# A streaming encoder trunk: the second block of frames turned once, the next frames' casts one per step, the pooled products later, one weight sum pinned

## The chip, the core and the metric

The kernel runs on one core of one Trainium2 chip. The metric is device microseconds of one execution. A TensorE matmul (PE) reads its operands from SBUF and adds into a bank of PSUM; VectorE (DVE) and ScalarE (ACT) prepare the operands and read the results; GpSimd (POOL) and SyncE (SP) mostly issue DMAs, and POOL computes a few small vectors. Each engine works off its own queue in order and waits on semaphores for the others.

## The reference

There are 2048 prompt frames and 32 sample frames of 1024 channels, and one layer:

```
proj = rmsnorm(h) @ w_in                   # 1024 -> 6 x 512: h, b, c, za, v, zb
u    = c * h ;  yA = b * (conv3(u) + bias) * silu(za)
pooled_g = (mean of the last 2/4/8/16 frames of v) - v        # four groups of 128 channels
yB   = (pooled_g @ pool_w_g) * pool_scale * silu(zb)
h    = h + concat(yA, yB) @ w_out
h    = h + (p @ w_ple) * sigmoid(rmsnorm(h) @ w_gate)
y    = rmsnorm(h)                          # and the last rows of u and v as new states
```

All inputs and outputs are fp32.

## The kernel before

**Tiling.** The 2080 frames are five blocks of 416, in groups [0, 1], [2, 3] and [4]. Channels run over the partitions, so the frames are loaded as rows, normalised (`normal`, L406) and turned by PE transposes through PSUM (`turn`, L413). fp32 products are made from pairs of parts: `split` casts a high part on ACT (L77) and subtracts it on DVE for the low part (L78), and each product is three matmuls (high x high, high x low, low x high). The trunk is: the projection by w_in (L556), the product with w_out (L162, L167), the embedding (L102), the gate, the last norm.

**Units.** The projection goes through four units of 128 columns of each of the six parts (h, b, c, za, v, zb) for each group. Unit 0 of group 0 is `plain`: six products for each block, zb, v, c, h, za, b. All other units of groups 0 and 1 are `seven`: three pairs (zb/v, c/h, za/b), each of which multiplies two blocks by two weights with seven half products (84 matmuls of 416 columns) instead of eight, as Strassen's scheme does. A `pair` is a generator of eight steps: weights, X with 11, Y with 12, X with the sum S2, Z with S1, X with S3, Z with S4, X with 22. `pair_weights` (L517) makes the sums of the raw weights on DVE (s_t is L536, the third sum is L533) and `make` splits them. X, Y and Z are PSUM banks (`ps_m`, six of them), emptied by ACT copies (`carry`, L851) and DVE additions (L854, L885). Group 1's unit 0 runs its zb/v and c/h pairs side by side, step for step. Group 2's four units are `plain` with one block.

**Frames for group 0.** Block 0's frames are turned at the start. `second_block` (L585) is a generator that `plain` calls between its products: it normalises block 1's frames, turns them into B0's parts 12 and 22 (pt1, in banks of `ps_m`), and later, for each of four column chunks (128, 128, 128 and 32 frames), turns the same frames a second time (pt2, in the two banks of `ps_t`), copies one half by ACT (L611) and forms the combinations T1, T2, T3, T4 with block 0's parts on DVE (L604). T4 goes to memory through a staging tile.

**Frames for group 1.** While units 1 to 3 run, `aside` is called 24 times a unit, at each step of each pair. It advances `next_columns(3, 0, 1, 2)` at a pace of 35 steps for 56 calls: for each column chunk, `frame_sums` (L431) takes the sums of squares on ACT (L88), normalises, turns, forms the sums f12, f1, f21 (L445 to L455) and stages each part: `to_memory` (L479) splits it into a staging tile of the ring `xin` (five buffers, shared with the loaded frames xt) and a POOL DMA stores it in p_d. The halves of the next chunk's frames are loaded by SP (L392) at its steps 5 and 7, counted from 0. `load_group(1)` loads the parts back by POOL.

**Pooling.** `pool_blocks` forms the trailing sums of v on DVE (L726, L735 to L738) and splits the result pl into pp. `mix` (L698) multiplies pp by pool_w, three matmuls for each block (L704 to L706), and DVE scales it into zs (L708); the result is stored in y_d by SP (L697).

**Order.** A scheduler orders the instructions of each engine's queue unless `keep_in_program_order` holds some of them in the order of the program. Before the change the turns of the next frames and the statistics of frames are so held.

Of the kernel before, what the change touches and what calls it, by code (L numbers as in the profile page):

```python
# [12 lines left out]
ALU = mybir.AluOpType  # L13
PSUM = bass.MemoryType.PSUM

P = 128
# [3 lines left out]
DEC = 32  # L20
# [7 lines left out]
NH = D // 2  # L28
KH = KC // 2
# [5 lines left out]
def trunk(ctx, tc, x_p, x_s, c_conv, c_pool, p_p, p_s, g_mix, w_in, conv_w, conv_b, pool_w,  # L35
          pool_scale, w_out, g_ple, w_gate, w_ple, g_fin, y_p, y_s, sc_p, sp_p, sc_s, sp_s):
    nc = tc.nc
# [38 lines left out]
    def split(hi, lo, src, eng=nc.vector):  # L76
        ins = nc.scalar.copy(hi, src)  # L77
        eng.tensor_tensor(lo, src, hi.bitcast(F32), op=ALU.subtract)  # L78
        return ins
# [250 lines left out]
    with ExitStack() as s1:  # L330
# [16 lines left out]

        def put(piece, src):

            split(piece[:, :, 0], piece[:, :, 1], src)  # L350

        def ftile(name):
            return wk.tile([P, KH, P], F32, tag="f", bufs=4, name=name)
# [42 lines left out]
        def x_stat(x, later=False):  # L396

            t, n, name = x
            return t, n, sumsq(t, n, name, later=later)
# [34 lines left out]
        def frame_sums(xs, tag, dst):  # L434

            xs = [x_stat(x, True) for x in xs]
            for x in xs:  # L440
                normal(x)
                yield
            n = P if len(xs) == 2 else DEC
            f12, f1, f21 = (ftile(f"{c}_{tag}")[:, :, :n] for c in ("f12", "f1", "f21"))
            sub = lambda o, x, y: nc.vector.tensor_tensor(o, x, y, op=ALU.subtract)  # L445
            steps = four(xs, tag)
            p11, p12 = next(steps)
            nc.scalar.copy(f12, p12)
            sub(f1, f12, p11)
            dst("11", p11, n)  # L450
            yield
            dst("T1", f1, n)
            yield
            p21, p22 = next(steps)
            nc.scalar.copy(f21, p21)  # L455
            sub(f1, p22, f1)
            sub(f12, p22, f12)
            dst("21", p21, n)
            yield
            dst("22", p22, n)  # L460
            yield
            dst("T2", f1, n)
            sub(f21, f21, f1)
            yield
            dst("T3", f12, n)
            yield
            dst("T4", f21, n)
            yield
# [7 lines left out]
        def staged(name):  # L476
            return xin.tile([P, KH, 2, P], F32R, tag="t", name=name)

        def to_memory(mem, name, src, at, n, t=None):  # L479
            t = t or staged(name)[:, :, :, :n]  # L480
            put(t, src)
            nc.gpsimd.dma_start(mem[:, :, :, at:at + n], t.bitcast(F32))

        def six(g):
# [39 lines left out]
        def pair_weights(gi, ka, kb, j, name, ring, s_ring):  # L524

            s_t = (wk.tile([P, KH, P], F32, tag="s", bufs=1, name=f"s_{name}") if s_ring is None else
                   s_ring(f"s_{name}"))  # L530
            ra = raw_weight(ka, j, f"{name}a", ring)
            a11, a12 = ra[:, :KH], ra[:, KH:]
            sub = lambda o, x, y: nc.vector.tensor_tensor(o, x, y, op=ALU.subtract)  # L533
            rb = raw_weight(kb, j, f"{name}b", ring)
            a21, a22 = rb[:, :KH], rb[:, KH:]
            nc.vector.tensor_tensor(s_t, a21, a22, op=ALU.add)  # L536
            sub(a21, a11, a21)
            s3 = a21
            src = {"11": a11, "12": a12, "S2": a11, "S1": s_t, "S3": s3, "S4": a12, "22": a22}

            def make(q):
                if q == "S2":
                    sub(a11, s_t, a11)
                if q == "S4":
                    sub(a12, a12, a11)
                t = wtile(f"w_{name}_{q}")
                put(t, src[q])
                return t

            return make  # L550
# [24 lines left out]
        B0 = {}  # L575
# [13 lines left out]
        def second_block():  # L589

            spans = [(c, slice(c * P, min(NB, c * P + P))) for c in range(4)]
            xs = []
            for c in range(3):
                x = x_tile(f"1_{c}", [x_rows(1, c)])
                normal(x)
                xs.append((x, slice(0, P)))
                yield
            xs.append((short0, slice(DEC, 2 * DEC)))
            for c, cs in spans:
                x = xs[c][0]  # L600
                for half, q in enumerate(("12", "22")):
                    put(B0[q][:, :, :, cs], turn(x, half, f"pt1_{c}_{half}", bank)[:, :, xs[c][1]])
                yield
            op = lambda o, a, b, op=ALU.subtract: nc.vector.tensor_tensor(o, a, b, op=op)  # L604
            for c, cs in spans:
                x, ts = xs[c]
                n = ts.stop - ts.start
                t1, t3, t2, t4 = (ftile(f"f{t}_1_{c}")[:, :, :n] for t in range(4))
                part = lambda q, h: B0[q][:, :, h, cs].bitcast(F32)
                p12 = turn(x, 0, f"pt2_{c}_0")[:, :, ts]  # L610
                nc.scalar.copy(t3, p12)  # L611
                op(t1, p12, part("11", 0))
                p22 = turn(x, 1, f"pt2_{c}_1")[:, :, ts]
                op(t3, p22, t3)
                op(t1, t1, part("11", 1))
                op(t2, p22, t1)
                put(B0["T2"][:, :, :, cs], t2)
                put(B0["T1"][:, :, :, cs], t1)
                put(B0["T3"][:, :, :, cs], t3)
                op(t4, part("21", 0), t2)  # L620
                op(t4, t4, part("21", 1), ALU.add)
                to_memory(p_d["T4"], f"T4_0_{c}", t4, c * P, n)
                yield
# [30 lines left out]
        class Unit:  # L654
# [98 lines left out]
            def plain(self):  # L753
# [73 lines left out]
                wb = weights("b", j, f"b{tag}")  # L827
                if self.last and j == 3:
                    early_embedding()
                for b in blocks:  # L830
                    ps = product_of("b", b, wb)
                    y = self.cols(c_s, b)
                    nc.vector.tensor_tensor(y, ps, y, op=ALU.mult)
                    self.store(j, b, c_s)
                if len(tbs) == 1:
                    self.turn_states(st)


            def pair(self, ka, kb, B, D, done, ring, s_ring=None):
# [39 lines left out]
            def seven(self, B, aside, both=False):  # L879
# [53 lines left out]
                while i < 3:  # L933
                    side_by_side = 2 if both and i == 0 else 1
                    if i <= 1 < i + side_by_side:
                        self.history(U, 2, halo_u, hist_u(j))
                    steps = [self.pair(*pairs[i + n], ring[i + n], ftile if n else None) for n in range(side_by_side)]
                    for _ in range(8):
                        for st in steps:
                            next(st)  # L940
                            aside()
                    for st in steps:
                        assert next(st, None) is None
                    i += side_by_side
                    if i - side_by_side <= 1 < i:
                        for b in range(2):
                            self.mix(b)

# [71 lines left out]
        def next_columns(*cs):  # L1020

            load_ahead(1, cs[0])
            for c, after in zip(cs, cs[1:] + (None,)):

                places = iter(t[:, :, :, i * DEC:(i + 1) * DEC] for t in map(staged, ("short_0", "short_1")) for i in range(4))
                dst = lambda q, src, n: to_memory(p_d[q], f"{q}_1_{c}", src, c * P, n, next(places) if n == DEC else None)
                for i, _ in enumerate(frame_sums(ahead.pop((1, c)), f"g1_{c}", dst)):
                    if after is not None and i in (5, 7):
                        load_half_ahead(after)
                    yield  # L1030

# [14 lines left out]
        def at_pace(steps, num, den):  # L1046

            calls = [0]

            def step():  # L1050
                calls[0] += num
                while calls[0] >= den:
                    calls[0] -= den
                    next(steps, None)

            return step

        B = B0
        for gi, tbs in enumerate(GROUPS):
# [17 lines left out]
            for j in range(4):  # L1077
                unit = gi * 4 + j
                u = Unit(gi, tbs, j)
                if unit == 0:  # L1080
                    u.plain()
                    B0["T4"] = piece_of(seventh("B0_T4"), 0)
                    nc.sync.dma_start(B0["T4"].bitcast(F32), p_d["T4"])
                    p_d["T4"] = tc.dram_tile([P, KH, 2, NB], F32, name="p_dT4b")
                    aside = at_pace(next_columns(3, 0, 1, 2), 35, 56)
                elif gi == 0:
                    u.seven(B, aside)
                elif gi == 1:
                    if j == 1:
                        aside = at_pace(last_block(), 1, 3)  # L1090
                    u.seven(B, aside, j == 0)
                else:
                    u.plain()
                if gi == 2:
                    early_sums(j)
# [403 lines left out]
```

## Time and profile before

| | us |
|---|---|
| median of 3 runs | 944.54 (944.16 to 944.74) |
| the profiled execution | 942.12 |
| its span, first to last instruction | 940.3 |
| ACT busy in the span | 480.5 |
| POOL busy in the span | 126.2 |

PE's granted clock is 0.994 of full speed over the span. A row of the order of time reads: start, time, engine, line, operation, tile written, tiles read, shape, count, and in brackets the idle time before it with what ended it. A row of the waits reads: instruction, what it waited for, us in total, times, longest. A row of a stretch reads: from:to in us, its length, the busy time of PE, PE's weight loads, DVE, ACT and POOL with the instruction counts (of PE alone where only PE was asked), the granted clock, the busy share of the DMA engines and GB/s. A row of the DMAs reads: destination, source, queue, count, KB each, median us from issue to landing. A row of the groups reads: instructions of one line and kind, busy time, mean ns of one, idle time before them.

### The profile page before, as it was taken

The numbers are of one execution on the slowest core, as the hardware profiler recorded it, in microseconds if no ns is written. First come the engines' busy times: TensorE is split into PE (matmuls) and PEld (weight loads), VectorE is DVE, ScalarE is ACT, GpSimd is POOL, SyncE is SP. The second block draws the span as 40 slices with busy tenths as digits, with TensorE's granted clock in tenths as the row PEclk, the third lists the DMA queues.
The fourth block names the chain that finished last, engine by engine and source line by source line (L and its number), as shares of the span: only waits on it lengthen the run. The fifth ranks groups of instructions, "written<-read, shape, count | busy, mean of one in ns | idle before, by whom it ended". The sixth has DMA issues, their size and how long they took to land.

```text
span 940.3 us, 13055 instructions
## 1 busy us (share of the span) xinstructions
PE 920.7 (98%) x4599; PEld 831.5 (88%) x4599; DVE 726.3 (77%) x1230; ACT 480.5 (51%) x890; POOL 126.2 (13%) x244
## 2 busy tenths in 40 slices
PE   7999999999999999999999999999999999999996
PEld 5999999999999999999999987888878868888885
DVE  6697998899587978785777588765554797888985
ACT  5554555454444554443454356334334875555564
POOL 2101222120000110000000010211211001211113
PEclk8999999999999999999999999999999999999999
DMA  8336586696952655418655359865785883566653
GB/s 247 101 105 172 143 243 197 182 255 207 423 166 80 178 161 144 151 52 287 198 167 176 117 176 305 263 194 170 217 253 171 307 274 130 201 227 209 216 207 112
DMA packets 133214, 182.96 MB, mean 195 GB/s; under 512 B 11164, under 2 KB 105116, under 8 KB 131869
## 3 DMA queue, kind: packets, MB, share of 16 engines
q1 hardware_dynamic: 117165, 131.70, 45.2%
q0 software_dynamic: 13248, 44.93, 14.9%
q10 hardware_dynamic: 2736, 5.51, 1.8%
q8 instruction: 36, 0.59, 0.3%
q14 instruction: 29, 0.24, 0.1%
HBM read 127.23 MB, written 54.86 MB: 194 GB/s over the span
## 4 chain that ended last, share of the span: by engine, by line
PE 74%; DMA 3%; DVE 2%; ACT 2%; issue 0%; POOL 0%; POOLq 0%; DVEq 0%; ACTq 0%
PE x_o L167 9%; PE x_g L167 9%; PE e L102 5%; PE z_g L167 5%; PE x_zab L556 5%; PE z_o L167 4%; PE x_ch L556 4%; PE x_zbv L556 4%; PE z_zab L556 2%; PE y_g L167 2%; PE y_o L167 2%; PE b L556 2%; PE v L556 2%; PE zb L556 2%; PE za L556 2%; PE c L556 2%
## 5 line engine op out<-in xcount | busy, mean ns | idle before, releaser
L77 ACT CAST y_S<-y_fS 128x512 fp32r<-128x512 f32 x32 | 19.5, 621 | 42.5 <-PE x_o L167 18.9
L102 PE MATMUL e<-wq,pps 128*128 128x512 f32 (+1 forms) x156 | 38.8, 399 | 0.2 <-ACT pps L77 0.2
L406 DVE SCALAR_TENSOR_TENSOR xt<-xt,rstd_x,g_bc 128x1024 f32<-128x1024 f32 (+2 forms) x18 | 23.1, 1282 | 19.4 <-POOL rstd_x L73 18.0
L167 PE MATMUL x_g<-wg_b,g_S 128*128 128x512 f32 x128 | 35.9, 390 | 0.0
L167 PE MATMUL x_o<-wo_b,y_S 128*128 128x512 f32 x128 | 35.8, 391 | 0.0
L556 PE MATMUL z_ch<-B,w_ch_S 128*128 128x416 f32 x168 | 34.3, 352 | 0.9 <-ACT U L851 0.9
L556 PE MATMUL z_zab<-B,w_zab_S 128*128 128x416 f32 x168 | 34.1, 351 | 0.5 <-ACT U L851 0.5
L556 PE MATMUL x_zab<-B,w_zab_S 128*128 128x416 f32 x168 | 34.5, 352 | 0.1
L556 PE MATMUL z_zbv<-B,w_zbv_S 128*128 128x416 f32 x168 | 34.2, 352 | 0.0
L556 PE MATMUL x_zbv<-B,w_zbv_S 128*128 128x416 f32 x168 | 34.1, 351 | 0.0
L556 PE MATMUL x_ch<-B,w_ch_S 128*128 128x416 f32 x168 | 34.0, 351 | 0.0
L102 PEld LDWEIGHTS e<-wq,pps 128*128 128x128 f32 (+1 forms) x156 | 27.4, 182 | 6.9 <-ACT pps L77 0.5
L556 PEld LDWEIGHTS z_ch<-B,w_ch_S 128*128 128x128 f32 x168 | 31.2, 188 | 1.6 <-ACT U L851 1.2
L556 PEld LDWEIGHTS z_zab<-B,w_zab_S 128*128 128x128 f32 x168 | 31.3, 188 | 1.1 <-ACT U L851 0.8
L556 PEld LDWEIGHTS x_zab<-B,w_zab_S 128*128 128x128 f32 x168 | 31.2, 188 | 1.0 <-DVE w_zab_S L78 0.4
L556 PEld LDWEIGHTS x_ch<-B,w_ch_S 128*128 128x128 f32 x168 | 31.4, 188 | 0.3
L556 PEld LDWEIGHTS x_zbv<-B,w_zbv_S 128*128 128x128 f32 x168 | 31.3, 188 | 0.3
L556 PEld LDWEIGHTS z_zbv<-B,w_zbv_S 128*128 128x128 f32 x168 | 31.3, 188 | 0.4
L69 POOL TENSOR_SCALAR ms_f<-ssq_f 128x1 f32<-128x1 f32 (+1 forms) x15 | 8.8, 585 | 160.7 <-ACT junk L88 160.7
L77 ACT CAST y<-y 128x512 fp32r<-128x512 f32 x24 | 14.8, 618 | 29.4 <-PE x_o L167 13.8
L1321 DVE SCALAR_TENSOR_TENSOR h<-h,rstd_f,g_bc 128x1024 f32<-128x1024 f32 (+1 forms) x15 | 19.3, 1284 | 12.7 <-POOL rstd_f L73 12.7
L167 PEld LDWEIGHTS x_o<-wo_b,y_S 128*128 128x128 f32 x128 | 24.0, 188 | 5.0 <-ACT c_o L1125 0.3
(570 smaller groups left out, 2670.7 us busy)
## 6 DMA issues: line engine op xcount, KB each, us to landing
y<-y_d SPq DMA_DIRECT2D x16, 512.0 KB, 12.7
x<-in_x_prompt_dram SPq DMA_DIRECT2D x16, 512.0 KB, 9.7
h_d<-x SPq DMA_DIRECT2D x16, 512.0 KB, 4.5
h<-h_d SPq DMA_DIRECT2D x16, 512.0 KB, 3.6
xt<-in_x_prompt_dram SPq DMA_DIRECT2D x15, 512.0 KB, 12.7
e<-e_d SPq DMA_DIRECT2D x15, 512.0 KB, 5.9
out_dram<-h POOLq DMA_DIRECT2D x14, 512.0 KB, 3.0
p_dT<-T POOLq DMA_DIRECT2D x12, 512.0 KB, 6.2
```

The source lines that it names most:

```text
L69: nc.gpsimd.tensor_scalar(ms[:n], ssq[:n], scalar1=1.0 / D, scalar2=EPS, op0=ALU.mult, op1=ALU.add)
L77: ins = nc.scalar.copy(hi, src)
L102: nc.tensor.matmul(ps[:n], pps[:, a, k, :n], wp[k][b][:, cs], start=k + q == 0, stop=k == 1 and q == 2)
L167: nc.tensor.matmul(ps[:n], lhs[:, k, a, :n], w[b][:, k], start=start and k + q == 0, stop=k == KH - 1 and q == 2, skip_group_check=True)
L406: nc.vector.scalar_tensor_tensor(xt[:n], xt[:n], r[:n], g_bc[:n], op0=ALU.mult, op1=ALU.mult)
L556: nc.tensor.matmul(ps[:, :NB], lhs[:, k, x], b[:, k, y], start=start and k + q == 0, stop=stop and k == KH - 1 and q == 2, skip_group_chec ...
L1321: nc.vector.scalar_tensor_tensor(h[:n], h[:n], rf[:n], g_bc[:n], op0=ALU.mult, op1=ALU.mult)
```

## The change

1. `second_block`: when block 1's frames are turned the first time, ACT also copies each result back into the tile xt of the frames. The combinations read these copies. The second turn (8 calls, 32 transposes) and the four copies of L611 go. ACT makes eight copies in place of four.
2. `next_columns` and `frame_sums`: a step between the statistics and the normalisation, so 39 steps instead of 35; the high casts of the parts that go to memory are held in program order; the second half of the next chunk's frames is loaded at step 6 or 7 rather than 5 or 7; the pace is 39 for 62 calls.
3. `seven`, in group 1's unit 0 alone: the two `mix` calls move from behind the side-by-side pairs to behind the third product step (S2) of the za/b pair.
4. `pair_weights`: the sum of a21 and a22 of the za/b weights in that unit is held in program order.
5. `plain` with one block (group 2): the turn of the states stands ahead of the b product.

PE has 32 instructions fewer (4567), ACT four more; DVE's, POOL's and SP's counts stay.

```diff
@@ frame_sums
             xs = [x_stat(x, True) for x in xs]
+            yield
             for x in xs:
                 normal(x)
                 yield
@@
-        def to_memory(mem, name, src, at, n, t=None):
+        def to_memory(mem, name, src, at, n, t=None, later=False):
             t = t or staged(name)[:, :, :, :n]
-            put(t, src)
+            ins = put(t, src)
+            if later:
+                tc.keep_in_program_order(ins)
             nc.gpsimd.dma_start(mem[:, :, :, at:at + n], t.bitcast(F32))
@@ pair_weights
-            nc.vector.tensor_tensor(s_t, a21, a22, op=ALU.add)
+            ins = nc.vector.tensor_tensor(s_t, a21, a22, op=ALU.add)
+            if (gi, ka, j) == (1, "za", 0):
+                tc.keep_in_program_order(ins)
@@ second_block
+            both = []
             for c, cs in spans:
-                x = xs[c][0]
+                x, ts = xs[c]
+                n = ts.stop - ts.start
+                both.append([x[0][:, half * NH:half * NH + KH * n].rearrange("p (k t) -> p k t", k=KH)
+                             for half in range(2)])
                 for half, q in enumerate(("12", "22")):
-                    put(B0[q][:, :, :, cs], turn(x, half, f"pt1_{c}_{half}", bank)[:, :, xs[c][1]])
+                    pt = turn(x, half, f"pt1_{c}_{half}", bank)[:, :, ts]
+                    put(B0[q][:, :, :, cs], pt)
+                    nc.scalar.copy(both[c][half], pt)
                 yield
@@
-                p12 = turn(x, 0, f"pt2_{c}_0")[:, :, ts]
-                nc.scalar.copy(t3, p12)
                 op(t1, p12, part("11", 0))
-                p22 = turn(x, 1, f"pt2_{c}_1")[:, :, ts]
-                op(t3, p22, t3)
+                op(t3, p22, p12)
@@ plain
+                if len(tbs) == 1:
+                    self.turn_states(st)
                 for b in blocks:
                     ps = product_of("b", b, wb)
...
-                if len(tbs) == 1:
-                    self.turn_states(st)
@@ seven
-                    for _ in range(8):
+                    for n in range(8):
                         for st in steps:
                             next(st)
                             aside()
+                        if both and i == 2 and n == 3:
+                            for b in range(2):
+                                self.mix(b)
...
-                    if i - side_by_side <= 1 < i:
+                    if i - side_by_side <= 1 < i and not both:
                         for b in range(2):
                             self.mix(b)
@@ next_columns
-                    if after is not None and i in (5, 7):
+                    if after is not None and i in (6, 7):
                         load_half_ahead(after)
@@
-                    aside = at_pace(next_columns(3, 0, 1, 2), 35, 56)
+                    aside = at_pace(next_columns(3, 0, 1, 2), 39, 62)
```

More of the change, by code (lines that the diff above doesn't have):

```diff
@@ L348, in put @@
         def put(piece, src):
-            split(piece[:, :, 0], piece[:, :, 1], src)
+            return split(piece[:, :, 0], piece[:, :, 1], src)
         def ftile(name):
@@ L605, in second_block @@
             for c, cs in spans:
-                x, ts = xs[c]
-                n = ts.stop - ts.start
+                p12, p22 = both[c]
+                n = cs.stop - cs.start
                 t1, t3, t2, t4 = (ftile(f"f{t}_1_{c}")[:, :, :n] for t in range(4))
                 part = lambda q, h: B0[q][:, :, h, cs].bitcast(F32)
-                p12 = turn(x, 0, f"pt2_{c}_0")[:, :, ts]
-                nc.scalar.copy(t3, p12)
                 op(t1, p12, part("11", 0))
-                p22 = turn(x, 1, f"pt2_{c}_1")[:, :, ts]
-                op(t3, p22, t3)
+                op(t3, p22, p12)
                 op(t1, t1, part("11", 1))
@@ L1025, in next_columns @@
                 places = iter(t[:, :, :, i * DEC:(i + 1) * DEC] for t in map(staged, ("short_0", "short_1")) for i in range(4))
-                dst = lambda q, src, n: to_memory(p_d[q], f"{q}_1_{c}", src, c * P, n, next(places) if n == DEC else None)
+                dst = lambda q, src, n: to_memory(p_d[q], f"{q}_1_{c}", src, c * P, n, next(places) if n == DEC else None, True)
                 for i, _ in enumerate(frame_sums(ahead.pop((1, c)), f"g1_{c}", dst)):
-                    if after is not None and i in (5, 7):
+                    if after is not None and i in (6, 7):
                         load_half_ahead(after)
```

## The prediction, made before the changed kernel had run

> **What bounds the kernel now.** I read the page first: its first rows, then the list of what TensorE (PE) waits for, then stretches of the span around those waits, then single rows in order of time.
>
> ```profile
> span 940.3 us, 13055 instructions
> PE 920.7 (98%) x4599; PEld 831.5 (88%) x4599; DVE 726.3 (77%) x1230; ACT 480.5 (51%) x890; POOL 126.2 (13%) x244
> PE pm L704 <- ACT pp L77: 1.6, 1, 1.6
> PE pt_g L413 <- DVE 11_1_2_1940 L78: 0.9, 1, 0.9
> PE z_ch L556 <- ACT U L851: 0.9, 1, 0.9
> PE z_zab L556 <- ACT U L851: 0.5, 1, 0.5
> ```
>
> PE is busy 98% of 940.3 us, so time is won only by taking work off PE or by closing one of its few waits; the other engines count only where they make PE wait. The profiled execution took 942.12 us, 1.8 of it outside the span and 2.4 less than the median of 944.54. The sum below is a difference, made in the span and then taken off that median.
>
> The named waits understate what they cost, because the ends of matmuls are modelled. Better is to compare a stretch with the pitch of its instructions.
>
> ```profile
> 276.05 1.68 PE L556 MATMUL y_zab<-B,w_zab 128*128 128x416 f32 x8
> 277.56 0.72 PE L556 MATMUL x_zab<-B,w_zab_S 128*128 128x416 f32 x3
> 61.87 1.03 PE L413 MATMUL pt<-ident,xt 128*128 128x128 f32 x8
> 62.66 0.43 PE L556 MATMUL za<-B,w_za 128*128 128x416 f32 x1
> 168.16:186.18 18.02, 17.49 (x94) 1.00 0.59 179
> 186.18:204.10 17.92, 16.98 (x94) 1.00 0.75 201
> 204.10:221.34 17.24, 16.38 (x85) 1.00 0.79 213
> 270.26:277.56 7.30, 5.75 (x30) 1.00 0.52 150
> ```
>
> Start to start, eight matmuls of 416 columns take 277.56-276.05 = 1.51 us, 0.189 each; eight transposes take 62.66-61.87 = 0.79. The last four rows are stretches of the span from one first matmul to another (length, PE's busy time, records that touch it). By the code each of the first three holds one pair of products by sevens, 7x12 = 84 matmuls (15.87 us), and the first two eight transposes as well (16.66). So they lose **(a)** 18.02-16.66 = 1.36 us in unit 2's za/b pair, **(b)** 17.92-16.66 = 1.26 in unit 3's zb/v pair, **(c)** 17.24-15.87 = 1.37 in unit 3's c/h pair. The fourth holds 29 matmuls (23 of zab, 6 of the pooled products), 5.48 us, and loses **(d)** 7.30-5.48 = 1.82 in group 1. That is 5.8 us, the listed waits among it.
>
> **The change part by part. 1: block 1 turned once.** Every removed transpose is on PE, between matmuls that follow without a gap. The first and the last of the four turns of four transposes, and the 64-wide one:
>
> ```profile
> 37.23 0.60 PE L413 MATMUL pt<-ident,xt 128*128 128x128 f32 x4
> 37.58 0.44 PE L556 MATMUL c<-B,w_firstc 128*128 128x416 f32 x1
> 54.05 0.60 PE L413 MATMUL pt<-ident,xt 128*128 128x128 f32 x4
> 54.40 0.44 PE L556 MATMUL h<-B,w_h 128*128 128x416 f32 x1
> 71.90 0.71 PE L413 MATMUL pt<-ident,xt 64*128 64x64 f32 x8
> 72.54 0.46 PE L556 MATMUL b<-B,w_b 128*128 128x416 f32 x1
> ```
>
> 37.58-37.23 = 0.35, four times 1.40; with the eight at 61.87 (0.79) and the short ones (0.64) **-2.83 us**, 32 transposes. The copies that replace them go to ACT and DVE:
>
> ```profile
> 36.12 0.46 PE L704 MATMUL pm<-pp,pw 128*128 128x416 f32 x1
> 38.04 1.30 PE L556 MATMUL zb<-B,w_firstzb 128*128 128x416 f32 x6
> 35.01 2.87 DVE L78 TENSOR_TENSOR B<-pt,B 128x512 fp32r<-128x512 f32 x6
> 38.48 0.69 DVE L604 TENSOR_TENSOR f<-pt,B 128x512 f32<-128x512 f32 x1
> 39.21 0.69 DVE L604 TENSOR_TENSOR f<-f,B 128x512 f32<-128x512 f32 x1
> 37.86 0.59 ACT L611 COPY f<-pt 128x512 f32<-128x512 f32 x1 [1.19 <-PE pt L413]
> ```
>
> ACT gets eight copies and loses four, 4x0.59 = 2.4 us spread over the 35 us of block 0, on an engine that is busy half of the span: nothing, its idle half is the cover, and without that cover the 2.4 us would be PE's. DVE has the same number of operations, and reading PSUM (f<-pt, 0.69) or SBUF (f<-f, 0.69) takes the same: nothing. The Trainium skill, "VectorE: DVE Perf Modes", Specifications, says VectorE sits closer to SBUF; if that made the moved operands cheaper, DVE's subtractions would end earlier and the new wait below would shrink. The two rows of 0.69 speak against it, and I give it nothing.
>
> What it does change is order. The first combinations of block 1 need no second turn any more, so two of them, which stood at 38.48 behind the six low-part subtractions of B (35.01, ending 37.88), now stand ahead of the last of these. Two at 0.6 (39.21-38.48 = 0.73 at most) put those 1.2 us later, and the zb matmuls that started at 38.04 need the last one. From 36.12 PE has then only the three pm and one each of zb, v and c (6x0.189 = 1.13 us), since the turn and one h that filled the place are gone. Done at 36.12+1.13 = 37.25, PE goes on at about 39.1 (38.04 and twice 0.6, less the turn's end that it no longer waits for): a **new wait of +1.85 us**. Bounds: 0 if the subtractions are served first, 2.45 if three combinations stand ahead (39.7-37.25). I take 1.85, nearest to the order of the changed program's queues. Later in block 0 nothing waits by that order: the weights for h and za are split about 2 us ahead of their matmuls. Net for part 1: **-1.0**.
>
> **2: casts one per step, pace 39/62.** Two of the three waits come from ACT's and DVE's queues.
>
> ```profile
> 177.50 1.06 ACT L88 ACTIVATE junk<-xt 128x1024 bf16<-128x1024 f32 x1
> 180.11 0.49 ACT L851 COPY U<-z_zab 128x416 f32<-128x416 f32 x1
> 189.26 0.68 DVE L78 TENSOR_TENSOR 11_1_2_1940<-pt_g,11_1_2_1940 128x512 fp32r<-128x512 f32 x1
> 210.31 0.69 DVE L536 TENSOR_TENSOR s_zab<-raw_zab_3b 128x512 f32<-128x512 f32 x1 [2.21 <-DMA raw_zab_3b<-in_w_in_dram]
> 215.11 0.89 ACT L77 CAST pp<-pl 128x832 fp32r<-128x832 f32 x1 [3.50 <-DVE pl L737]
> ```
>
> (a) The copy of U, which frees z_zab's bank, stood at 180.11 behind the two statistics of the next frames begun at 177.50. (b) The second turn of frames (pt_g) waited for a bank until the split at 189.26 had read the first. (c) DVE waited 2.21 us for raw_zab_3b, so the pooled sums were late, ACT's cast of them stood 3.50 us, and U's copy behind it. In the changed queues the statistics stand a step later than that copy, each turn has its casts in its own step, and raw_zab_3b is issued about 10 us earlier. All three go: **-1.36 -1.26 -1.37 = -4.0**. Bounds for each: 0 to the whole.
>
> What is late next: 39 steps over 62 calls instead of 35 over 56 bring two turns of frames into x_ch's third sum of unit 2, by 0.6 us before the normalisation of the frames is done: **+0.6** (0 to 1.28, one normalisation). And the load of the last frames' second half. SP now has it behind the two y_d stores.
>
> ```profile
> 158.79 8.51 SPq L392 DMA_DIRECT2D xt<-in_x_prompt_dram  x2
> xt<-in_x_prompt_dram SPq DMA_DIRECT2D x15, 512.0 KB, 12.7
> xt<-in_x_prompt_dram SPq DMA_DIRECT2D x2, 512.0 KB, 18.6
> raw_ch_3a<-in_w_in_dram SPq DMA_DIRECT2D x1, 512.0 KB, 3.8
> L406 DVE SCALAR_TENSOR_TENSOR xt<-xt,rstd_x,g_bc 128x1024 f32<-128x1024 f32 (+2 forms) x18 | 23.1, 1282 | 19.4 <-POOL rstd_x L73 18.0
> ```
>
> Its issue goes from about 167 (158.79+8.51) to about 173.5. Statistic (1.06) and normalisation (1.28) of it stand ahead of the split of w_zbv's second sum, which PE wants near 188.3 by the new times (186.18-1.0-1.36, and 24 matmuls of 0.189); with the other casts and subtractions that stand between, about 7 us from landing to product, a landing up to 181.2 costs nothing, and each us later costs PE one. Landings took from 3.8 (a weight in the same stage) over 12.7 (median of all xt) to 18.6 us (a later stage): landing at 177.3, 186.2 or 192.1, cost 0, 5.0 or 10.9. I take the first, since the frames' and pooled blocks' transfers are through by then, with +0.7 for the part of that risk that is small delays.
>
> **3 and 4: pooled products later, third sum pinned.**
>
> ```profile
> 273.91 1.02 DVE L78 TENSOR_TENSOR pp<-pl,pp 128x832 fp32r<-128x832 f32 x1
> 250.00:275.00 25.00, 23.45 (x125) 22.87 (x124) 15.68 (x26) 10.67 (x19) 0.00 (x0) 1.00 0.72 264
> ```
>
> The first pm waited 1.6 us for ACT's cast of the pooled sums (the list above), the others for their low part, which ends at 274.93. The six pm now come after 36 matmuls of the za/b pair, 270.26+36x0.189 = 277.1, so both are ready some 2 us ahead: **-1.82** (bounds 0 to that). The pinned sum costs DVE nothing more (15.68 of 25 busy); the sums it orders are done 2.5 us or more ahead of their products. SP's load of the next c/h weights goes about 7 us later with the order, and has some 10 us left.
>
> **5: group 2's states turned earlier.** The same 24 matmuls, moved within PE's queue: 0, the b product behind them being ready either way.
>
> **Sum:** -1.0 -4.0 +0.6 +0.7 -1.8 = **-5.5 us**, carried to the end, since PE, busy 98% of the span, bounds what follows too. Profile 936.6, median 944.5-5.5 = **939.0**.
>
> **Rivals.**
>
> ```profile
> 175.00:200.00 25.00, 23.59 (x130) 22.42 (x129) 23.80 (x41) 16.37 (x32) 8.30 (x11) 1.00 0.52 149
> 0.00:24.00 24.00, 17.12 (x63) 13.27 (x64) 15.31 (x25) 13.12 (x25) 5.76 (x45) 0.86 0.88 249
> ```
>
> *R1, the waits move.* From 175 to 200 DVE is busy 23.80 of 25 us (the third sum of a row, after PE and its weight loads), and with PE's stretches 4 us shorter the same work must fit in less. Then one or two of (a) to (c) come back elsewhere: -5.5+2.7 = -2.8, 941.7. For it: three different waits in a row, each by queue order. Against: ACT is busy only 16.37 of the 25, and two of the three were ACT's order. *R2, nothing gained.* The change doesn't do what it says, to free the queues: the new wait has its upper bound (-2.83+2.45 = -0.4), (a) to (c) return, only (d) goes, and 0.6+0.7 is lost: -0.9, 943.6. *R3, slower, by one transfer.* The second half of the last frames lands 18.6 us after issue: a stall of 10.9 us, -5.5-0.7+10.9 = +4.7, 949.2. It decides from a landing of 181.2+6.2 = 187.4 on, 13.9 us after issue; the 12.7 row stands near it, the 3.8 row in the same stage against it.
>
> The granted clock is 0.86 in the first 24 us, where PE has gaps; around the 1.6 us wait for pp it stayed 1.00 (the row 250:275 above), so the new wait should not lower it. The Trainium skill, "TensorE: Matmul & The Clock Gate", The HAM clock gate, says that about 3.4 us idle halve the clock until as long a busy time. By that rule R3's stall would cost some 1.7 us more, as an estimate, 950.9; no row of before has such a gap after the start.
>
> **How the numbers follow.** Forecast 0.60 (936 to 941), R1 0.20, R2 0.11, R3 0.09. What this kernel's measurement can tell from no change is about 0.2%, 1.9 us. Faster by more: 0.60+0.20+0.02 of R2 = 0.82; within: 0.09; slower: 0.09. The range goes down to 936.0 (the new wait 0.6 shorter, and neither the turns of frames nor the load late: -1.6-4.0-1.8 = -7.4, 937.1, and 1.1 for the spread of a median against a profile) and up to 943.4, which takes in R1 with an end of -1.1 and leaves out R3 and most of R2.
>
> **What would show it.** Right: 32 fewer pt transposes; a gap of 1 to 2 us ahead of zb near 38; the four stretches at 16.7, 16.7, 15.9 and, with the pm moved, no gap ahead of pm; the 250:275 stretch busy to 24.5 or more. Wrong: a wait of PE for DVE's subtraction of a w_zbv_S or of the last frames near 188 (R3), or waits of z_ or pt_g of 1 us and more between 150 and 221 (R1); a gap of over 2.5 us at 38, or none, would say that I misjudged the queue of the first block.

## The result, and the profile after

| | before | changed |
|---|---|---|
| median | 944.35 us (943.69 to 944.74, 4 runs) | 938.76 us (937.85 to 940.76, 4 runs) |
| profiled execution | 942.12 | 940.76 |
| its span | 940.3 | 939.0 |

The ratio is 0.9944, with a 95% interval of 0.9928 to 0.9960, which is 5.3 us; the medians differ by 5.6 us, against a forecast of 5.5. Two more measurements of the same kernel, below, gave 0.9955 and 0.9946. So the number was right. The two profiled executions differ by only 1.4 us, though, and what they show is not what the prediction added up. That was the question for the experiments.

The first rows of the changed kernel's page, and then three rows of its list of PE's waits:

```profile
span 939.0 us, 13008 instructions
PE 918.3 (98%) x4567; PEld 829.4 (88%) x4567; DVE 727.4 (77%) x1230; ACT 482.2 (51%) x894; POOL 129.3 (14%) x244
```

```profile
PE pt_g L413 <- DVE xt L406: 1.8, 2, 1.2
PE zb L561 <- ACT B L77: 1.7, 1, 1.7
PE x_zab L561 <- ACT V L859: 0.5, 1, 0.5
```

The four waits of before (pm, the first pt_g, z_ch, z_zab) are gone, and these three are new. The same stretches as the prediction's, by their first matmuls (unit 2's c/h pair, unit 2's za/b, unit 3's zb/v and c/h, then the 60 us around group 1's unit 0), in the changed kernel:

```profile
149.50:169.42 19.92, 18.14 (x102) 1.00 0.32 92
169.42:187.25 17.83, 17.38 (x93) 1.00 0.91 279
187.25:205.16 17.91, 17.87 (x102) 1.00 0.54 157
205.16:222.24 17.08, 17.08 (x93) 1.00 0.85 242
240.00:300.00 60.00, 60.00 (x321) 1.00 0.67 233
```

and the one of them that the prediction didn't show, in the kernel before:

```profile
150.21:168.16 17.95, 17.95 (x101) 1.00 0.76 225
```

A pair is 84 matmuls, 15.87 us; the changed kernel adds sixteen transposes (1.59), six pm (1.13), sixteen transposes and six pm to the four. The loss against the pitch is 2.46, 0.83, 0.45 and 0.08 us, 3.8 together. Before it was 0.16 (84 matmuls, six pm and eight transposes), 1.36, 1.26 and 1.37, 4.15 together. So (a), (b) and (c) went (their pairs still lose 0.83, 0.45 and 0.08), and more than half of what they had cost came back one pair earlier. (d) is gone with nothing in its place: the last row is busy throughout.

At the start the new wait is there, and behind it something the prediction had ruled out. PE in order of time, and then the same place in stretches of 2 us:

```profile
36.85 0.35 PE L714 MATMUL pm<-pp,pw 128*128 128x416 f32 x1
38.94 0.65 PE L561 MATMUL zb<-B,w_firstzb 128*128 128x416 f32 x1 [1.74 <-ACT B L77]
39.39 0.55 PE L561 MATMUL v<-B,w_firstv 128*128 128x416 f32 x1
39.74 0.55 PE L561 MATMUL c<-B,w_firstc 128*128 128x416 f32 x1
```

```profile
36.00:38.00 2.00, 1.20 (x10) 1.00 0.00 0
38.00:40.00 2.00, 1.06 (x3) 0.76 0.00 0
40.00:42.00 2.00, 2.00 (x7) 0.50 0.32 111
42.00:44.00 2.00, 2.00 (x11) 0.89 0.00 0
```

PE waits 1.74 us (1.85 were forecast), and then the granted clock is down to 0.50 for 3.41 us, from 39.04 to 42.45: the matmuls stand 0.35 us apart instead of 0.19.

### The profile page after: what moved, and what is told of

The parts are those of the page before. It is cut to its first block, busy times and chain, and to the rows that moved or that the text cites. A ratio compares the mean times of both kernels' runs of the same rounds, so it can differ in the third digit from the quotient of the medians.

```text
span 939.0 us, 13008 instructions
## 1 busy us (share of the span) xinstructions
PE 918.3 (98%) x4567; PEld 829.4 (88%) x4567; DVE 727.4 (77%) x1230; ACT 482.2 (51%) x894; POOL 129.3 (14%) x244
## 4 chain that ended last, share of the span: by engine, by line
PE 79%; ACT 1%; DMA 1%; DVE 1%; POOL 0%; issue 0%; POOLq 0%; SPq 0%; ACTq 0%
PE x_o L167 9%; PE x_g L167 9%; PE x_zab L561 5%; PE x_ch L561 5%; PE x_zbv L561 5%; PE e L102 5%; PE z_g L167 5%; PE z_o L167 4%; PE z_ch L561 3%; PE z_zab L561 3%; PE z_zbv L561 2%; PE y_g L167 2%; PE y_o L167 2%; PE b L561 2%; PE za L561 2%; PE c L561 2%
## 5 line engine op out<-in xcount | busy, mean ns | idle before, releaser
L77 ACT CAST y<-y 128x512 fp32r<-128x512 f32 x24 | 14.8, 618 | 29.6 <-PE x_o L167 13.7
```

## The experiments

The theory behind the prediction was: four independent gains, each a wait taken away, less one new wait. The rivals were R1 (the waits move), R2 and R3. After the result a further one stood: the parts are not independent, and the drop of the clock has its own price. In the tables below "unit 0" is the time from the row of 24 transposes (block 1's first turn) to the first matmul of unit 1, "units 1 to 3" goes from there to group 1, and "g1u0" is group 1's unit 0; all are differences of start times in the traces.

**Both kernels again.**

> The kernel before, once more, to see how much its traces differ from one another. If the four waits (a) to (d) are fixed by the queues' order, they return at the same places: 0.4 to 0.5 us for z_zab, 0.9 for pt_g, 0.9 for z_ch and 1.5 for pm, and a median near 944.4. If an idle of PE of 1.5 us and more now and then costs a drop of the granted clock (in the changed kernel's trace 1.74 us ahead of zb at 38.94 is followed by a clock of 0.50 from 40 to 42), a trace of before may show such a drop behind the 1.55 us wait for pm near 273.9, and be some 1 to 2 us longer than the first trace's 942.12.

> The changed kernel, once more. Its first trace took 940.76 us, 2 more than its median of 938.76. If the drop of the clock behind the wait near 38.9 is by chance, this trace has it not, stays at 1.00 there, and takes 938 to 939; if the wait always brings it, the clock is 0.5 there again. The waits of pt_g for the normalised frames near 161 and 163 (1.16 and 0.62) come back if the queues' order makes them, and differ if the landing of the frames does.

> The changed kernel once more, on the same chip as the kernel beside it, so that the two can be compared: a ratio to the kernel before of 0.9955 as in its second run, 0.9940 to 0.9970.

| | ratio to before | unit 0 | units 1 to 3 | g1u0 |
|---|---|---|---|---|
| before, first trace | | 48.07 | 156.63 | 50.55 |
| before2 | 1.0007 (0.9993 to 1.0021) | 48.07 | 157.96 | 52.80 |
| changed, first trace | 0.9944 (0.9928 to 0.9960) | 48.08 | 156.13 | 48.72 |
| after2 | 0.9955 (0.9939 to 0.9971) | 46.63 | 156.65 | 48.72 |
| after3 | 0.9946 (0.9925 to 0.9966) | 46.60 | 156.80 | 48.72 |

In after2 and after3 the same 1.7 us of waiting cost no clock. In before2 the clock fell behind the wait for pm, which was 2.25 us this time:

```profile
274.08 0.75 PE L704 MATMUL pm<-pp,pw 128*128 128x416 f32 x2 [2.25 <-ACT pp L77]
```

and by stretches of 2 us (from:to, length, PE busy, granted clock):

```profile
272.00:274.00 2.00, 0.00 (x0) 1.00 0.18 53
274.00:276.00 2.00, 1.92 (x6) 0.62 0.82 238
276.00:278.00 2.00, 2.00 (x7) 0.53 0.75 221
```

That unit then took 52.80 us instead of 50.55: 0.7 by the longer wait, some 1.5 by the clock. So (d) was worth 1.8 us in one execution and 4.1 in another, and the two first profiles stood at opposite ends: before's without a drop at (d), the changed kernel's with one at 39.

**Part 1 alone, part 2 alone.** p1_turned_once has the edit of `second_block` and nothing else; p2_casts_paced has this:

```diff
             xs = [x_stat(x, True) for x in xs]
+            yield
...
+            if later:
+                tc.keep_in_program_order(ins)
...
-                    if after is not None and i in (5, 7):
+                    if after is not None and i in (6, 7):
...
-                    aside = at_pace(next_columns(3, 0, 1, 2), 35, 56)
+                    aside = at_pace(next_columns(3, 0, 1, 2), 39, 62)
```

> Part 1 alone (block 1 turned once), all else as before. By the prediction's working -2.83 for 32 transposes and +1.85 for the new wait near 38: -1.0, a median near 943.4. Rival: with a drop of the clock behind the wait in each execution the gain is gone, 0 to +0.3, 944.4 to 944.7. (a) to (d) stay in both.

> Part 2 alone (the next frames' casts one per step, 39 steps for 62 calls). By the prediction's working -4.0 for the waits (a), (b), (c), +0.6 for the turns in unit 2 and +0.7 for the load: -2.7, a median near 941.7. Rival, from the changed kernel's trace, in which units 1 to 3 together take only 0.5 us less than before because the turns wait for the normalised frames near 161: -0.5, near 943.9.

| | ratio to before | unit 0 | units 1 to 3 | g1u0 |
|---|---|---|---|---|
| p1_turned_once | 1.0018 (1.0001 to 1.0035) | 46.63 | 158.09 | 50.54 |
| p2_casts_paced | 1.0091 (1.0067 to 1.0115) | 48.09 | 156.87 | 61.43 |

Neither part is a gain by itself. Part 1 takes 1.45 us from unit 0 (1.0 were forecast) and gives 1.2 back in unit 1 (52.85 us instead of 51.67 and 51.74). Its trace shows where, in order of time:

```profile
101.47 1.06 ACT L88 ACTIVATE junk<-xt 128x1024 bf16<-128x1024 f32 x1 [0.25 <-DMA xt<-in_x_prompt_dram]
103.04 0.49 ACT L854 COPY c_s<-x_ch 128x416 f32<-128x416 f32 x1
103.58 2.53 PE L556 MATMUL x_ch<-B,w_ch_S 128*128 128x416 f32 x12 [0.29 <-ACT c_s L854]
```

PE waits for ACT's copy of a bank, which stands behind a statistic of the next frames, and that had waited for their load. It is the order of (a) in another unit. The same product waits 1.15 us in no_paced_casts below, the other kernel that has part 1 without part 2, and there unit 1 takes 53.76 us. Part 2, forecast at 2.7 us less, costs 8.6. PE's wait, the two DVE operations that it waited for, and the issues of the load and of the group's frames, all in order of time on their engines:

```profile
262.25 3.83 PE L559 MATMUL z_ch<-B,w_ch_S 128*128 128x416 f32 x10 [10.07 <-DVE w_ch_S L78]
260.90 0.69 DVE L539 TENSOR_TENSOR s_zab<-raw_zab_0b 128x512 f32<-128x512 f32 x1 [22.23 <-DMA raw_zab_0b<-in_w_in_dram]
261.51 0.69 DVE L78 TENSOR_TENSOR w_ch_S<-s_ch,w_ch_S 128x512 fp32r<-128x512 f32 x1
226.56 0.95 SPq L511 DMA_DIRECT2D raw_zab_0b<-in_w_in_dram  x1
224.91 1.09 POOL L499 DMA_DIRECT2D B<-p_d  x2 [8.19 <-PE y_zab L559]
```

and the same load in the kernel before:

```profile
240.02 0.69 DVE L536 TENSOR_TENSOR s_zab<-raw_zab_0b 128x512 f32<-128x512 f32 x1
226.35 0.38 SPq L508 DMA_DIRECT2D raw_zab_0b<-in_w_in_dram  x1
227.48 1.10 POOL L496 DMA_DIRECT2D B<-p_d  x2 [27.72 <-PE y_zab L556]
```

DVE stood 22 us at one sum, which PE needed only in the za/b pair (first matmul at 275.46 in that trace), and behind that sum stood the subtraction that PE needed next. The load of that weight had been issued 1.65 us behind the first of the seven loads of group 1's frames, where before it had gone 1.13 us ahead of them. Ahead, it was there within 13.7 us; behind, it took 34. The trace of before doesn't show this wait, since the load came early there; what can be read beforehand is that s_zab stands ahead of w_ch_S on DVE.

**The changed kernel less one part.** no_pin is the changed kernel without part 4, no_late_pool without part 3, no_paced_casts without part 2. This is the edit of no_pin:

```diff
-            ins = nc.vector.tensor_tensor(s_t, a21, a22, op=ALU.add)
-            if (gi, ka, j) == (1, "za", 0):
-                tc.keep_in_program_order(ins)
+            nc.vector.tensor_tensor(s_t, a21, a22, op=ALU.add)
```

> The changed kernel without part 4 (the sum of the za/b weights in group 1's unit 0 is not held in program order). Part 2 alone took 8.5 us more than before, with one wait of 10.07 us of z_ch for the low part of w_ch_S, which stood on DVE behind the sum s_zab, and that sum behind the load of raw_zab_0b. Theory: the pin is what takes s_zab from ahead of that subtraction, so the wait comes back here, 8 to 10 us, with a drop of the clock behind it, and the time is near 948 to 950. The prediction's working gave the pin nothing: by that, the time of the changed kernel, 938 to 939. Rival: the later pooled products (part 3) have moved the order of DVE by themselves, also 938 to 939.

> The changed kernel without part 3 (the pooled products stand where they stood). Theory: the wait for the cast of pp comes back, 1.5 to 2.3 us, and in some executions a drop of the granted clock behind it of about 1.5 us, as in the second trace of before (clock 0.53 to 0.62 from 274 to 278): 1.8 to 3.3 us more than the changed kernel. Rival: with the pinned sum behind it on DVE the pooled sums come early enough, and the time is the changed kernel's.

> The changed kernel without part 2: parts 1, 3, 4, 5. By the prediction's working part 2 is worth 2.7 us, so 2.7 more than the changed kernel. By the traces units 1 to 3 took 156.6 and 158.0 us before, 156.1 and 156.7 in the changed kernel, but 158.1 with part 1 alone, which loses 1.2 us in unit 1: 1.5 to 2 us more than the changed kernel. Rival: part 2 is worth nothing there, or costs, since its turns wait for the normalised frames in unit 2: the same or less time.

| | ratio to before | units 1 to 3 | g1u0 |
|---|---|---|---|
| no_pin | 1.0084 (1.0063 to 1.0104) | 158.40 | 60.86 |
| no_late_pool | 1.0013 (0.9999 to 1.0027) | 157.09 | 54.57 |
| no_paced_casts | 0.9974 (0.9960 to 0.9989) | 159.02 | 48.72 |

One line, the pin, carries 13 us (951.49 against 938.43, medians taken beside kernels before of 942.08 and 941.93). Without it the wait of part 2 is back, with the clock at half behind it. A row of the list of PE's waits, and then a stretch of 6 us:

```profile
PE z_ch L559 <- DVE w_ch_S L78: 9.9, 1, 9.9
```

```profile
258.00:264.00 6.00, 0.85 (x2) 0.50 0.77 250
```

The pin puts s_zab behind w_ch_S on DVE. raw_zab_0b comes as late as in part 2 alone (the last of its packets starts 33 to 34 us behind the issue in the changed kernel's three traces), but nothing waits for it. The price of the pin is that all sums of the za/b weights come late, and this is what part 3 pays for. Without it, PE waits for them behind the pooled products, and takes the next twelve matmuls at a lower clock (4.27 us to the next row):

```profile
279.10 4.44 PE L561 MATMUL x_zab<-B,w_zab_S 128*128 128x416 f32 x12 [3.44 <-ACT w_zab_S L77]
283.37 2.43 PE L561 MATMUL z_zab<-B,w_zab_S 128*128 128x416 f32 x12
```

That is 944.58, 6 us more than the changed kernel, and not the return of (d) that I expected: pm waits no more, the sums do. And part 2, in the company of 3 and 4, is worth 0.9974-0.9955 = 0.0019 of the time, 1.8 us of the 2.7 forecast. The intervals of these two ratios overlap; the traces give 2.5 us in units 1 to 3 (159.02 against 156.53, the mean of the changed kernel's three).

**Why units 1 to 3 gave so little.** In after2 unit 2 holds the turn that the prediction priced at 0.6 us. PE's rows, then ACT's and DVE's of the frames that they turn:

```profile
153.63 1.22 PE L561 MATMUL x_ch<-B,w_ch_S 128*128 128x416 f32 x5
156.01 0.63 PE L413 MATMUL pt_g<-ident,xt 128*128 128x128 f32 x4 [1.16 <-DVE xt L406]
156.39 1.02 PE L561 MATMUL x_ch<-B,w_ch_S 128*128 128x416 f32 x4
158.01 0.63 PE L413 MATMUL pt_g<-ident,xt 128*128 128x128 f32 x4 [0.60 <-DVE xt L406]
151.25 0.89 ACT L77 CAST pp<-pl 128x832 fp32r<-128x832 f32 x1 [1.55 <-DVE pl L745]
152.04 1.05 ACT L88 ACTIVATE junk<-xt 128x1024 bf16<-128x1024 f32 x1
154.58 1.28 DVE L406 SCALAR_TENSOR_TENSOR xt<-xt,rstd_x,g_bc 128x1024 f32<-128x1024 f32 x1 [0.72 <-POOL rstd_x L73]
```

The frames had been issued at 130 and 134 us; they were not late. Their statistics stood on ACT behind the cast of the pooled sums, which stood 1.55 us for DVE: the same pattern as (c), in another unit. It is also the sign of R1 that the prediction had named, a wait of pt_g of 1 us or more between 150 and 221. Two attempts to move the turn away added a step between normalisation and turn:

```diff
                 normal(x)
                 yield
+            yield
...
-                    if after is not None and i in (6, 7):
+                    if after is not None and i in (7, 8):
...
-                    aside = at_pace(next_columns(3, 0, 1, 2), 39, 62)
+                    aside = at_pace(next_columns(3, 0, 1, 2), 43, 68)      # step_before_turn
+                    aside = at_pace(next_columns(3, 0, 1, 2), 43, 62)      # step_same_end
```

> The changed kernel with one more step between the normalisation and the turn of each chunk of the next frames (43 steps for 68 calls, the loads at steps 7 and 8). In the traces of the changed kernel PE waits 1.16 and 0.60 us in unit 2 for the normalised frames, with gaps of 2.3 us in all against the pitch; ACT's statistics stood there behind the cast of the pooled sums, which waited for DVE. If that is only the turn being asked for too early, one step more removes it: 1.5 to 2.3 us less than the changed kernel, 936 to 937. If the order of the saturated DVE sets it, the wait moves to another place and the time is the same or longer.

> The step between normalisation and turn once more, with the pace that ends the chunks where the changed kernel ends them (43 steps for 62 calls instead of 68). With 68 calls, units 1 to 3 took 153.1 us instead of 156.1 and 156.7, but the loads of the next group's weights were issued among its frames' loads and one came 28 us late. Theory: that lateness came from the later end alone; with 62 the order of SP's loads is the changed kernel's, group 1's unit 0 takes 48.7 us again, and units 1 to 3 gain 1 to 3 us: 935.5 to 937.5. Rival: the turns fall on the busy DVE again and units 1 to 3 take as long as in the changed kernel, 938 to 939.

| | ratio to before | units 1 to 3 | g1u0 |
|---|---|---|---|
| step_before_turn | 1.0219 (1.0198 to 1.0240) | 153.06 | 78.62 |
| step_same_end | 0.9984 (0.9972 to 0.9996) | 160.48 | 48.72 |

With the later end units 1 to 3 were the fastest of all, by 3 us, and the loss behind them was ten times that: PE waited 28.08 us for a weight whose load stood behind the first of group 1's frames. With the earlier end that wait was gone, as expected, but PE lost 2.19 us at x_ch in unit 2, with 3.41 us of half clock behind it, and 0.9 at x_zbv in unit 3. That is 941.53 us in all, more than both the theory (935.5 to 937.5) and the rival (938 to 939) had said. So the pace has to serve both, and no run here had both.

**The new wait filled.** early_h issues the first half of block 0's h product ahead of block 1's zb, v and c; early_h_other_bank is the same with `tbank` for `bank`:

```diff
                         if b == 0:
+                            self.history(U, 2, halo_u, hist_u(j))
+                            wh = weights("h", j, f"h{tag}")
                             for _ in range(3):
                                 next(second)
+                            ph = bank(f"h{tag}_{tbs[0]}")
+                            half_product(ph, wh[0], hn[tbs[0]][0], True, False)
...
+                    if len(tbs) > 1 and b == 0:
+                        half_product(ph, wh[1], hn[tbs[0]][1], False)
+                        ps = ph[:, :NB]
```

> The changed kernel with one edit in unit 0: the first half of block 0's h product (12 matmuls, 2.27 us) is issued ahead of block 1's zb, v and c, with its weights. PE waits there 1.74 us for ACT's cast of the last columns in each trace of the turned-once kernels, and the granted clock fell to 0.5 behind that wait in four of seven of them. Theory: the 12 matmuls fill the wait, 1.7 us less, no drop of the clock before 60 us in this trace, and by the share of the drops (about 1.2 us each) some 0.6 us more on the median: 2 to 2.5 us less than the changed kernel, near 936. Rival: what PE waits for moves back with the 12 matmuls (the banks, DVE's low parts), and the gain is under 0.5 us.

> As the kernel with the early first half of h, but h accumulates in one of the two banks of the pooled products instead of one of the six that the turned frames fill. In the trace of that kernel the 12 matmuls waited 1.07 us for ACT to copy a turned block out of its bank. Theory: that wait is the bank's, it goes, and the time is 1.1 us less than with the early h alone: 935.5 to 936.5. Rival: zb then waits for the same copies and low parts, and the time is that of the early h, about 937.

| | ratio to before | unit 0 |
|---|---|---|
| early_h | 0.9943 (0.9925 to 0.9960) | 45.86 |
| early_h_other_bank | 0.9921 (0.9899 to 0.9944) | 45.16 |

In early_h the gain over the changed kernel is 0.1 to 1.1 us by the ratios, less than the 2 to 2.5 expected and not clear of their intervals. The twelve matmuls themselves waited, for one of the six banks that the turned frames held (first row below, in order of time). In the other bank they follow the transposes at once (next three rows, of early_h_other_bank), and from 24 to 60 us PE is busy for 35.96 of 36 us (last row).

```profile
36.17 2.54 PE L561 MATMUL h<-B,w_h 128*128 128x416 f32 x12 [1.07 <-ACT xt L613]
```

```profile
30.36 2.55 PE L413 MATMUL pt<-ident,xt 128*128 128x128 f32 x24
32.84 2.53 PE L561 MATMUL h<-B,w_h 128*128 128x416 f32 x12
35.41 4.95 PE L561 MATMUL zb<-B,w_firstzb 128*128 128x416 f32 x24
```

```profile
24.00:60.00 36.00, 35.96 (x203) 1.00 0.32 88
```

935.31 us, beside 937.72 for the changed kernel on the same chip (after3), is the shortest time of the study; the intervals of the two ratios (0.9899 to 0.9944 and 0.9925 to 0.9966) overlap a little, so the 2.4 us between them are likely but not shown. One trace of each has 46.60 and 45.16 us for unit 0.

## Why the prediction was right, and where it was not

**The total was right, by terms that were not.** Worked out from the traces, before's two against the changed kernel's three:

| step | forecast | traces |
|---|---|---|
| part 1, unit 0 | -1.0 | -1.45 without a drop of the clock, 0 with one |
| units 1 to 3: (a) to (c) less the turns and the load | -2.7 | -0.8 (156.53 against 157.30, means) |
| parts 3 and 4, (d) | -1.8 | -1.83 and -4.08, mean -2.95 |
| part 5 | 0 | 0 (217.3 us from group 1's unit 2 to the product with w_out in all five) |

With clean clocks in unit 0 that is -5.2. Behind group 1's unit 0 the changed kernel's traces are 0.4 us longer (652.06 against 651.62, means), which nothing here explains. The three measurements give 4.2 to 5.3 us less by their ratios, 3.5 to 5.6 by their medians. Too much credit for part 2 was made up by (d) and part 1, so the closeness of 5.5 to 5.6 is partly luck.

**Part 1: the gain was there, the wait came from another engine.** 32 transposes went, the wait is 1.74 us where 1.85 was forecast, and unit 0 gained 0.36 us more than the two together give. I put the wait behind the first matmul of zb and gave DVE's low part as its cause; it stands ahead of that matmul and is released by ACT's cast of the last columns, behind the added copies. I said that the ACT copies cost nothing. Four of them, 2.3 us, stand ahead of that cast: before, ACT's casts of these frames were done at 36.68, 3.04 us behind the start of the 24 transposes; now the one that PE waits for ends at 38.88, 4.99 us behind it. In early_h the h product waits 1.07 us for one of them. So the term put at nothing is what PE waits for, and that 1.74 lies so near to 1.85 is luck. I also looked no further than unit 0, and part 1 without part 2 loses 1.2 to 2.1 us in unit 1.

**Part 2: the step that failed is "all three go".** The three waits did go; which step of the edit took each was not tried singly. That their place would stay empty except for 0.6 us of turns did not hold: the pair with the turns loses 2.46 us. A reading that fits the traces, but is not proved by them, is this: with DVE busy for 23.8 of 25 us, a pooled block and a turn in the same pair wait for one another, and the change only picks the pair in which they meet. Moving the turns by a step took 3 us off units 1 to 3 with one pace and added 4 with the other. That was R1, with a chance of 0.20; it came in units 1 to 3, where it took 1.9 us (-0.8 instead of -2.7) of the 2.7 it was priced at, and the total still came out as forecast. The -0.8 is not part 2's worth beside the other parts, which is 2.5 by no_paced_casts: part 2 also takes away what part 1 would lose in unit 1.

**The late load (R3) did not come.** No trace of the changed kernel has PE waiting for the last frames' second half near 188. What was late instead was the next group's weight, 34 us in flight, and part 4 kept it off the path.

**Part 4: "costs DVE nothing more" was right, and missed the point.** I weighed what the pin adds and not what the queue would be without it. Undone alone it costs 13 us, part 3 undone alone 6: the parts are not a sum of gains, but each repairs what another has broken. A prediction of part 2 alone by my terms would have been wrong by 11 us.

**The clock: "the new wait should not lower it" failed.** Of the nine traces with the 1.7 us wait (the changed kernel's three and six of the variants) five show the drop, a clock of 0.95 from 24 to 60 us, and four don't. Unit 0 takes 46.60 to 46.63 us in the four, 47.87 to 48.18 in the five: 1.4 us for a drop. One row at 1.00, behind a wait of 1.55 us, had been too little to conclude from. Which of the nine show the drop can be read from the traces (last section).

Open: how much of a 3.41 us interval PE may stand idle before the clock falls, and whether the frames' load is all that part 1 alone loses 1.2 us to in unit 1; neither was tried by itself.

## What to carry to other kernels

When a change has several parts, ask of each what the queues are without it: here a pin priced at nothing carried 13 us, because another part had put a load behind a burst of transfers. A wait removed from an engine beside a nearly full one (DVE, 95% in those stages) can come back at the next meeting of the same two jobs; count the loss of whole stretches against the pitch, not the named waits. And fill a gap on PE with independent matmuls if there are any, with a bank of their own, since a gap of 1.7 us may cost 1.4 us more in clock.

## What the runs showed of the hardware

**A wait of 1.7 us can halve the granted clock, depending on where it falls in a grid of 3.41 us.** Five of nine waits of 1.72 to 1.74 us, and one of 2.25 us, were followed by a clock of 0.50 for 3.41 us; a wait of 1.55 us was not. Within each of the fourteen traces any two changes of the clock stand a whole multiple of 3.41 us apart. So they lie on a grid, and where the grid lies against the program differs from trace to trace. These are two such intervals of the changed kernel's first trace, with the drop, and then two of after2, without one (PE alone):

```profile
35.62:39.04 3.42, 1.68 (x14) 1.00 0.01 2
39.04:42.45 3.41, 3.41 (x10) 0.50 0.19 65
30.82:34.23 3.41, 2.60 (x22) 1.00 0.01 2
34.23:37.65 3.42, 2.50 (x13) 1.00 0.18 62
```

In the first trace the whole wait lies in one interval; in after2 0.81 us of it lie in one and 0.92 in the next. In the five traces with the drop 1.35 to 1.74 us of the wait lay ahead of the grid's next point, and the clock fell at that point; in the four without it was 0.30 to 1.19 us. The wait's length alone is not the rule: before's 1.55 us for pm lay whole in one interval, among matmuls and not behind 24 transposes, and brought no drop, while in no_pin waits of 1.22 and 0.55 us in one interval of unit 2 did. All this is read off the traces; no run tried it by itself.

The Trainium skill, "TensorE: Matmul & The Clock Gate", The HAM clock gate, gives an idle window of about 3.4 us for the fall and as much sustained work for the return. The length of the window and the return agree with these traces (0.50 from 40 to 42, 0.89 from 42 to 44, 1.00 after). The fall does not: it came where PE stood idle for as little as 1.35 us of such a window, and the measurement decides.

**A load of small rows behind large ones gets one row for each large packet.** In part 2 alone the DMAs from 240 to 256 us, and then those from 256 to 261, were, by queue (POOL's is q0, SP's q1: packets, MB, share of the engines' time):

```profile
q0 software_dynamic: 534, 6.42, 96.1%
q1 hardware_dynamic: 534, 0.27, 5.7%
```

```profile
q1 hardware_dynamic: 1595, 1.44, 90.7%
q0 software_dynamic: 38, 0.29, 14.2%
```

While both queues have work, each moves as many packets as the other, and SP's carry one row of 512 bytes each (0.27 MB in 534). The Trainium skill, "DMA: Bandwidth & Descriptors", Queues, rings and completion order, says that an engine takes turns between its queues packet by packet. These rows agree.

POOL's packets took 0.961x16x16/534 = 0.46 us each. Half a weight, 512 KB in rows of 512 bytes, is 64 rows for each of 16 engines, so behind such a burst it needs about 64x0.46 = 29 us, as an estimate. That is what raw_zab_0a took, issued 0.6 us ahead of raw_zab_0b in the same queue: its last packet started at 256.91, 31 us behind its issue. The rows of raw_zab_0b started only then, and went in 3.3 us, since POOL's burst was over by 258. So its 34 us are the wait for the half ahead of it and for the end of the burst.
